# Spreading the S5 parameters over the first feed-forward blocks, and the zeros for the inverses' DRAM blocks over the output stage behind them

## The chip, the cores and the metric

The kernel runs on one core of one Trainium2 chip. The metric is the device time of one execution in microseconds (us). The kernel before was run three times: 1168.38, 1169.02 and 1170.4 us, median 1169.02 us.

## The reference, cut to what matters

One layer of a backbone is computed for 384 tokens of width 1024 (128 context tokens and 256 latent tokens, which share the weights). The order is: norm, SwiGLU feed-forward, norm, a mixer of three branches (S5, SSD, gated DeltaNet), norm, SwiGLU feed-forward, final norm. Each norm's scale and shift and each residual's gate come from an "ada" projection of the condition.

```python
mod = (jax.nn.silu(cond) @ p['ada_w'] + p['ada_b']).reshape(cond.shape[0], 1, N_ADA, D_MODEL)
h = _rmsnorm(x, p['norm_g'][0]) * (1.0 + sc1) + sh1
x = x + 0.5 * g1 * _swiglu(h, p['ffn_wi'][0], p['ffn_wo'][0])
...
# in the S5 branch, from weights alone
dt = jnp.exp(log_dt)[:, None]
mag = jnp.exp(lam_re * dt)
lb_re = mag * jnp.cos(lam_im * dt)
lb_im = mag * jnp.sin(lam_im * dt)
cr = ((lb_re - 1.0) * lam_re + lb_im * lam_im) / den
bb_re = cr[..., None] * b_re - ci[..., None] * b_im
```

The change touches only work that depends on weights and conditions, not on the tokens: these S5 parameters (the powers of the complex decay and the scaled input matrices), the silu of the conditions from which later ada sections are made, and a block of zeros in DRAM which the DeltaNet inverses later fill in part.

## The kernel before, in words

**Matrix products.** Each f32 weight tile of 128 x 1024 is read by DMA into one of three `wraw` buffers and split in two (`split_w`, L279 to L286): ScalarE writes the high part `whi` (L284), VectorE the low part `wlo` (L285). Two buffers each hold `whi` and `wlo`. TensorE makes three products for each 128-row slice (`mm3`, L291 to L293): high by high, high by low, low by high, so 24 matmuls of 384 columns for a weight of 8 slices.

**The first norm** (`modnorm`, L365 to L381) goes through eight slices of the activations in four sections of two. Ahead of a section, `sections` calls `ada_first` (L212 to L233): four DMAs of ada weights (`araw`, L217), matmuls (L221), a copy on ScalarE (L224), transposes (L227), a reduction and an addition on VectorE (L229, L233). Then come `mscale` (L343), the scaled tokens `nt` (L376, VectorE), the high part `hh` (L378, ScalarE) and the low part `hl` (L379, VectorE). The first feed-forward blocks consume slices as they come.

**The first feed-forward** (`ffn`, L389 on) has two parts. In each, 11 blocks m make the two halves of the SwiGLU from two weights (`wi`), multiply (`g`, L409) and split (`gh`, L418; `gl`, L419); m counts from 0 to 21 over both parts. Then an output stage of 8 blocks multiplies with `wo` and adds to x (L431). Behind each block's `gl` stands a call of `fill(m, g)`, behind each output block one of `fill2(part, m)`, both inside `tc.issue_after(last.ins)`: each instruction of VectorE that is traced inside is queued behind that block's last VectorE instruction. Instructions of other engines, and DMA issues on SP's queue, get no such edge.

**Side work in the fills.** `rest` is the generator `ada_rest` (L257 to L274) for three more ada sections. Its first step reads the conditions `cb` (1 MB, broadcast to all partitions, L262), held back by a VectorE copy of one element (L261), and takes their silu on ScalarE (L263). Each of its 24 steps then reads one `araw` (L268) and makes two VectorE products with it (L271). `tables` (`s5_tables`, L549 on) makes eight pairs of S5 tables in two steps each: E (L566 to L572), then B with transposes, matmuls and small copies on top. There are 16 steps.

**Ahead of the fills**, behind the first norm in the program: `zr` is made on GpSimd as zero times the norm's last `hl` (L1337), so that its DMA to `dI` in DRAM (1.5 MB, L1338) can't start earlier; and `s5_params` (L470 to L547) makes the S5 parameters from `smalls` (the second parameter DMA, L1334) by chains of small VectorE instructions on 128 x 32 values, with Exp (L479, L481) and Sin (L494, L497) on ScalarE, reads `braw` and `craw` (L532, L535, each held by a one-element copy of `hl`), and multiplies `bb` (six products of 128 x 512, by `cmul`, L460 to L468).

**Order.** The instructions of each engine stand in an order that is settled when the program is built, by a list scheduler with a model of times: an instruction whose inputs and buffers are there can be placed ahead of others that stand before it in the program. Each engine then works through its order. All DMAs of this stage are issued from SP's one queue.

## Time and profile before

| | |
|---|---|
| median of three runs | 1169.02 us |
| the profiled execution's own time | 1170.72 us |
| its span | 1168.9 us |
| busy: TensorE, VectorE, ScalarE, GpSimd | 1104.1, 807.4, 458.0, 200.3 us |
| mean granted TensorE clock | 0.974 of full speed |
| moved by DMA | 199.21 MB, 170 GB/s over the span |

The span counts from the first to the last instruction of the profiled execution; 1.8 us of its time lie outside. In the rows below PE is TensorE's matmuls and PEld its weight loads, DVE is VectorE, ACT is ScalarE, POOL is GpSimd, SPq is the queue from which SP issues DMAs. A row of the timeline gives the start, the duration, the engine, the line, the operation with output and inputs, the count, and in brackets the idle time of that engine just before, with what ended it. Matmuls are pipelined: each starts before the recorded end of the one before it, so the distance of starts is what one costs.

### The profile page before, as it was taken

What the parts mean: (1) busy time and instruction counts of PE and PEld (TensorE: products, weight loads), DVE (VectorE), ACT (ScalarE), POOL (GpSimd) and SP (SyncE); (2) the same over time, 40 slices, a digit from 0 to 9 for tenths busy, and PEclk for the clock granted to TensorE, in tenths of its full rate; (3) what the DMA queues carried; (4) which work ended last, traced back from release to release, by engine and by line L of the source; (5) the groups of instructions that cost most, each with busy time, mean ns of one, the idle gap of its engine ahead of it and who ended that gap; (6) DMA issues with size and microseconds to landing.
All of it is one profiled execution on the core that took longest, in us unless ns stands there. A gap on an engine that the chain in (4) does not pass through costs nothing.

```text
span 1168.9 us, 19259 instructions
## 1 busy us (share of the span) xinstructions
PE 1104.1 (94%) x7264; PEld 1039.9 (89%) x7264; DVE 807.4 (69%) x1698; ACT 458.0 (39%) x774; POOL 200.3 (17%) x270
## 2 busy tenths in 40 slices
PE   5899999999998999889699999999999999999996
PEld 2689999999998998778588888999899999999996
DVE  4699987997657589954564567775775984455554
ACT  5353333333545573553333222334354433234341
POOL 0000000000000008881372552113500000000000
PEclk9999999999998899989799999999999999999998
DMA  9786767555655353248746444365764644444342
GB/s 355 266 265 213 224 212 234 167 167 161 225 167 145 123 164 112 75 124 245 207 138 216 153 120 125 130 201 163 226 195 145 201 130 122 142 126 127 104 124 80
DMA packets 107342, 199.21 MB, mean 170 GB/s; under 512 B 35056, under 2 KB 61936, under 8 KB 106992
## 3 DMA queue, kind: packets, MB, share of 16 engines
q1 hardware_dynamic: 107248, 197.98, 54.6%
q8 instruction: 57, 0.93, 0.3%
q14 instruction: 37, 0.30, 0.1%
HBM read 175.56 MB, written 22.38 MB: 169 GB/s over the span
## 4 chain that ended last, share of the span: by engine, by line
PE 75%; DVE 12%; DMA 4%; issue 3%; ACT 3%; POOL 2%; SPq 1%; DVEq 0%; ACTq 0%; POOLq 0%
PE ps_d L293 20%; PE ps_d L291 20%; PE ps_d L292 20%; DVE wlo L285 2%; ACT whi L284 1%; DVE sc L818 1%; DMA wraw<-in_win_dram 1%; PE ps_c L1032 1%; PE ps_d L243 1%; PE ps_s L770 1%; PE ps_m L221 1%; PE ps_s L1032 1%; PE ps_m L849 1%; DVE cv L679 1%; DVE Ss L822 1%
## 5 line engine op out<-in xcount | busy, mean ns | idle before, releaser
L284 ACT CAST whi<-wraw 128x1024 fp32r<-128x1024 f32 (+3 forms) x247 | 227.9, 924 | 466.9 <-PE ps_d L292 306.4
L285 DVE TENSOR_TENSOR wlo<-wraw,whi 128x1024 fp32r<-128x1024 f32 (+3 forms) x247 | 276.3, 1119 | 120.8 <-ACT whi L284 119.7
L291 PE MATMUL ps_d<-hh,whi 128*128 128x384 f32 x696 | 243.1, 350 | 16.2 <-ACT whi L284 13.2
L293 PE MATMUL ps_d<-hh,wlo 128*128 128x384 f32 x696 | 243.7, 351 | 5.5 <-DVE wlo L285 5.4
L292 PE MATMUL ps_d<-hl,whi 128*128 128x384 f32 x696 | 242.2, 348 | 0.6 <-DVE hl L379 0.6
L291 PEld LDWEIGHTS ps_d<-hh,whi 128*128 128x128 f32 x696 | 134.4, 193 | 25.9 <-ACT whi L284 16.8
L293 PEld LDWEIGHTS ps_d<-hh,wlo 128*128 128x128 f32 x696 | 135.0, 194 | 12.8 <-DVE wlo L285 9.7
L292 PEld LDWEIGHTS ps_d<-hl,whi 128*128 128x128 f32 x696 | 135.1, 194 | 3.3 <-issue 1.8
L291 PE MATMUL ps_d<-xh,whi 128*128 128x386 f32 x352 | 120.0, 341 | 0.0
L293 PE MATMUL ps_d<-gh,wlo 128*128 128x384 f32 x352 | 119.1, 338 | 1.0 <-DVE wlo L285 1.0
L293 PE MATMUL ps_d<-xh,wlo 128*128 128x386 f32 x352 | 119.9, 341 | 0.0
L291 PE MATMUL ps_d<-gh,whi 128*128 128x384 f32 x352 | 118.8, 337 | 0.4 <-ACT whi L284 0.4
L292 PE MATMUL ps_d<-xl,whi 128*128 128x386 f32 x352 | 118.9, 338 | 0.0
L292 PE MATMUL ps_d<-gl,whi 128*128 128x384 f32 x352 | 118.6, 337 | 0.0
L271 DVE SCALAR_TENSOR_TENSOR ajunk<-araw,cb 128x1024 bf16<-128x1024 f32 x64 | 77.8, 1215 | 1.6 <-ACT cb L263 1.6
L293 PEld LDWEIGHTS ps_d<-gh,wlo 128*128 128x128 f32 x352 | 66.0, 188 | 2.0 <-DVE wlo L285 1.6
L291 PEld LDWEIGHTS ps_d<-gh,whi 128*128 128x128 f32 x352 | 66.1, 188 | 0.9 <-ACT whi L284 0.7
L292 PEld LDWEIGHTS ps_d<-xl,whi 128*128 128x128 f32 x352 | 66.6, 189 | 0.0
L293 PEld LDWEIGHTS ps_d<-xh,wlo 128*128 128x128 f32 x352 | 66.2, 188 | 0.2 <-DVE wlo L285 0.2
L291 PEld LDWEIGHTS ps_d<-xh,whi 128*128 128x128 f32 x352 | 66.3, 188 | 0.0
L292 PEld LDWEIGHTS ps_d<-gl,whi 128*128 128x128 f32 x352 | 66.1, 188 | 0.0
L431 DVE SCALAR_TENSOR_TENSOR x<-ps_d,gate,x 128x128 f32<-128x128 f32 x64 | 23.7, 412 | 29.3 <-PE ps_d L293 29.3
(466 smaller groups left out, 1821.1 us busy)
## 6 DMA issues: line engine op xcount, KB each, us to landing
wraw<-in_wi_dram SPq DMA_DIRECT2D x88, 512.0 KB
wraw<-in_win_dram SPq DMA_DIRECT2D x50, 512.0 KB
araw<-in_ada_dram SPq DMA_DIRECT2D x48, 512.0 KB
wraw<-in_wo_dram SPq DMA_DIRECT2D x32, 384.0 KB
wraw<-in_ada_dram SPq DMA_DIRECT2D x24, 512.0 KB
wraw<-in_wo_dram SPq DMA_DIRECT2D x32, 320.0 KB
wraw<-in_wbr_dram SPq DMA_DIRECT2D x32, 256.0 KB
dM<-sgate SPq DMA_DIRECT2D x24, 192.0 KB
```

Of the source, the lines that this page charges most:

```text
L221: PE.matmul(pt[32 * g:32 * g + 32, :], c32[:, k, :], raw[:, j, :], start=q < 2, stop=q >= 2, tile_position=(0, 32 * g))
L243: PE.matmul(pt[32 * g:32 * g + 32, :], c32[:, 4 * h + g, :], raw[:, g, :], start=h == 0, stop=h == 1, tile_position=(0, 32 * g))
L271: V.scalar_tensor_tensor(junk, raw, 1.0, cb[:, e], op0=ALU.mult, op1=ALU.mult, accum_out=t[:, b, e:e + 1])
L284: S.copy(hi, raw)
L285: V.tensor_tensor(lo, raw, hi.bitcast(F32), op=ALU.subtract)
L291: PE.matmul(pt, hi[:, k, :], xh[k0 + k], start=start and k == 0, stop=False)
L292: PE.matmul(pt, hi[:, k, :], xl[k0 + k], start=False, stop=False)
L293: PE.matmul(pt, lo[:, k, :], xh[k0 + k], start=False, stop=stop and k == nk - 1)
L431: last = V.scalar_tensor_tensor(xv[m][:, s0:s1], py[:, s0:s1], gate[:, m, e:e + 1], xv[m][:, s0:s1], op0=ALU.mult, op1=ALU.add)
L679: V.scalar_tensor_tensor(ol, il, ws, ol, op0=ALU.mult, op1=ALU.add)
L770: PE.matmul(pt[:, ri, g], sw[:, ri, g], UU[:, 4 * b + g], start=True, stop=True)
L1032: PE.matmul(dst[r_, h], lh[r_, h], rh[r_, h] if len(rh.shape) == 3 else rh[r_], start=True, stop=True)
```

## The change

`s5_params` becomes part of the generator `tables`: it is no longer run behind the first norm, but in four steps (three inner `yield`s and one before its return) inside `fill`, ahead of the first table. `tables` now takes a step at every block but m = 11, where it skipped six blocks before. `rest` takes its first eight steps at m = 2 to 9, where they were at m = 0 to 7, and so the conditions' read comes with m = 2. `zr` is set by a plain memset without the norm's `hl` as input. The one DMA of 1.5 MB of zeros becomes four of 384 KB, in `fill2` behind output blocks 0, 2, 4 and 6 of part 0.

```diff
 def s5_params(sp, after):
...
         S.activation(cs, ab, AF.Sin)
+        yield
         pw = sp.tile([P, 2, 10, 32], F32, name="pw")
...
         V.tensor_copy(mu[:, 1, 1], pw[:, 0, 8])
 
+        yield
         den, t1, t2, cr, ci, lm = (t32() for _ in range(6))
...
         cmul(V, bb[:, 0, :, 0:16], bb[:, 1, :, 0:16], braw[:, 0], braw[:, 1], crb, cib, b1, b2)
 
+        yield
         pq = sp.tile([P, 2, 10, 32], F32, name="pq")
...
         V.tensor_copy(pb[64:128], pw[64:128, :, 0:8])
+        yield
         return bb, craw, pq, pb
...
-        zr = s5pool.tile([P, 256], F32, name="zr")
-        G.tensor_scalar(zr, hl[KD - 1][:, 0:256].bitcast(F32), 0.0, None, op0=ALU.mult)
-        nc.sync.dma_start(out=dI.rearrange("t d x h p c -> (t d x h p c)").rearrange("(n p c) -> p n c", p=P, c=256), in_=zr.unsqueeze(1).to_broadcast([P, 12, 256]))
-        tabs = s5_params(s5pool, hl[KD - 1].bitcast(F32))
-
         rest = ada_rest(s5pool, (2, 3, 4), hl[KD - 1].bitcast(F32))
 
         def all_tables():
+            tabs = yield from s5_params(s5pool, hl[KD - 1].bitcast(F32))
             for b in range(8):
                 yield from s5_tables(s5pool, b, *tabs)
 
         tables = all_tables()
+        zr = s5pool.tile([P, 256], F32, name="zr")
+        G.memset(zr, 0.0)
 
         def fill(m, g):
-            if m < 8 or 11 <= m < 19:
+            if 2 <= m < 10 or 11 <= m < 19:
                 next(rest, None)
-            if m not in (0, 5, 9, 11, 16, 20):
+            if m != 11:
                 next(tables, None)
 
         def fill2(part, m):
             if part == 0:
                 next(rest, None)
+                if m % 2 == 0:
+                    m //= 2
+                    nc.sync.dma_start(out=dI.rearrange("t d x h p c -> (t d x h p c)").rearrange("(n p c) -> p n c", p=P, c=256)[:, 3 * m:3 * m + 3],
+                                      in_=zr.unsqueeze(1).to_broadcast([P, 3, 256]))
```

## Rows read from the trace of the kernel before

**Rows 1.** The page, busy time and share of the span of each engine.

```profile
PE 1104.1 (94%) x7264; PEld 1039.9 (89%) x7264; DVE 807.4 (69%) x1698; ACT 458.0 (39%) x774; POOL 200.3 (17%) x270
```

**Rows 2.** Busy time by stretch (length, engines, granted clock, DMA share, GB/s).

```profile
24.00:40.00 16.00, 12.43 (x59) 7.25 (x59) 15.58 (x81) 7.24 (x16) 0.00 (x0) 0.79 0.98 384
...
62.00:141.00 79.00, 75.66 (x492) 74.03 (x493) 77.14 (x121) 32.60 (x50) 0.00 (x0) 1.00 0.75 237
...
190.00:283.00 93.00, 91.11 (x604) 88.78 (x608) 81.18 (x123) 33.46 (x50) 0.00 (x0) 1.00 0.57 177
```

**Rows 3.** Timeline, 20 to 38 us: the first norm's first two sections.

```profile
20.49 0.19 DVE L229 TENSOR_REDUCE at<-ps_m 128x8 f32<-128x32 f32 x1 [5.42 <-PE ps_m L227]
...
21.27 1.40 DVE L376 SCALAR_TENSOR_TENSOR nt<-x,mscale,rb 128x128 f32<-128x128 f32 x4
...
26.18 0.18 DVE L514 TENSOR_TENSOR s5t<-smalls 128x32 f32<-128x32 f32 x1
...
31.22 0.18 DVE L229 TENSOR_REDUCE at<-ps_m 128x8 f32<-128x32 f32 x1
...
32.12 0.23 DVE L233 TENSOR_TENSOR mod<-at,smalls 128x4 f32<-128x4 f32 x2
...
33.14 1.39 DVE L376 SCALAR_TENSOR_TENSOR nt<-x,mscale,rb 128x128 f32<-128x128 f32 x4
...
35.23 0.96 PE L227 MATMUL ps_m<-ident,arows 128*128 128x128 f32 x4
35.73 1.01 DVE L379 SCALAR_TENSOR_TENSOR hl<-nt,mod,hh 128x128 fp32r<-128x128 f32 x3
...
36.53 0.69 PE L292 MATMUL ps_d<-hl,whi 128*128 128x384 f32 x1 [0.34 <-DVE hl L379]
...
37.74 0.49 DVE L544 COPY pq<-pw 64x640 f32<-64x640 f32 x1
```

**Rows 4.** Groups of VectorE by line, 26 to 38.3 us.

```profile
L379 DVE SCALAR_TENSOR_TENSOR hl<-nt,mod,hh 128x256 fp32r<-128x256 f32 (+1 forms) x5 | 2.0, 427 | 0.0
```

**Rows 5.** Timeline, 66 to 78 us: blocks 3 and 4 and the conditions' silu.

```profile
66.34 0.34 PE L291 MATMUL ps_d<-hh,whi 128*128 128x384 f32 x1
...
68.56 0.33 SPq L262 DMA_DIRECT2D cb<-in_condr_dram  x1
...
70.55 0.34 PE L291 MATMUL ps_d<-hh,whi 128*128 128x384 f32 x1
...
74.68 1.91 ACT L263 ACTIVATE cb<-cb 128x2048 f32<-128x2048 f32 x1 [2.62 <-DMA cb<-in_condr_dram]
...
75.13 1.22 DVE L285 TENSOR_TENSOR wlo<-wraw,whi 128x1024 fp32r<-128x1024 f32 x1
...
76.50 1.03 ACT L284 CAST whi<-wraw 128x1024 fp32r<-128x1024 f32 x1
...
77.58 0.44 PE L291 MATMUL ps_d<-hh,whi 128*128 128x384 f32 x1 [2.30 <-ACT whi L284]
```

**Rows 6.** Groups of VectorE by line, 62 to 141 us.

```profile
L285 DVE TENSOR_TENSOR wlo<-wraw,whi 128x1024 fp32r<-128x1024 f32 (+1 forms) x18 | 21.7, 1203 | 4.0 <-ACT whi L284 4.0
...
L566 DVE TENSOR_TENSOR tE<-craw,pq 128x640 f32<-128x640 f32 x6 | 4.7, 818 | 0.0
```

**Rows 7.** Timeline: GpSimd's first memsets, SP's queue to 60 us.

```profile
1.26 1.81 POOL L529 MEMSET bb<- 128x2048 f32 x1
...
12.68 0.33 SPq L1334 DMA_DIRECT2D smalls<-in_small_dram  x1
14.59 7.68 SPq L217 DMA_DIRECT2D araw<-in_ada_dram  x6
...
58.29 0.38 SPq L1338 DMA_DIRECT2D dI<-zr  x1
```

**Rows 8.** Timeline, ScalarE at 24 us: a table load and the Exp behind it.

```profile
24.22 1.28 ACT L479 ACT_TABLE_LOAD   x1
25.51 0.23 ACT L479 ACTIVATE s5t<-smalls 128x32 f32<-128x32 f32 x1
```

## The prediction

> **What bounds the kernel now.** I read the page's busy times first: TensorE is busy 94% of the span [rows 1], so only work that reaches TensorE as idle time counts. Next I read the busy time by stretch. From 62 to 141 us, where blocks m = 3 to 10 run, TensorE is busy 75.66 of 79 us and idle 3.3, and VectorE is busy 77.14: two engines are full there, TensorE only just the fuller one in effect. From 24 to 40 us TensorE is busy 12.43 of 16 us at a granted clock of 0.79, between its two levels of 1.2 and 2.4 GHz, and DMA runs at a 0.98 share [rows 2]. So the start has idle TensorE time to give, and the feed-forward has little VectorE time to take.
>
> The timeline shows what fills VectorE at the start. The S5 chains run from 26.18 to 38.23 us in between the norm's own instructions [rows 3]. Sections 0 and 1 of the norm do the same steps: in section 0 it is 0.78 us from the reduction (20.49) to the first `nt` (21.27); in section 1 it is 1.92 us (31.22 to 33.14), as S5 products stand in between. After `nt` ends at 34.53, `hl` starts only at 35.73, behind S5 copies, and TensorE's product with it waits until 36.53 [rows 3].
>
> **The change, part by part.**
>
> *S5 chains leave the start.* Section 1 gains 1.92 - 0.78 = 1.1 us up to `nt` and 35.73 - 34.53 = 1.2 us behind it: `hl` could be there 2.3 us sooner. TensorE can't follow by all of that: four transposes (35.23, 0.96 us) stand ahead of its product [rows 3] and need the next section's DMA and a ScalarE copy, which moves by 1.1 us with `nt`. I take -1.5 us. The bounds are -2.7 (both VectorE delays and the wait of 0.34 that the row shows) and 0 (the DMA, at a share of 0.98 [rows 2], is late next).
>
> *The same chains enter the feed-forward.* Their stretch of 12.05 us holds 15 instructions of the norm: five `hl` at 2.0 us [rows 4], four `nt` at 1.39 [rows 3], and six small ones at no more than 0.23 each, 0.9 in all. So the S5 part is 12.05 - 4.3 = 7.8 us of VectorE. It now comes behind blocks 0 to 3. Against it, one table step fewer is due by m = 10 (seven steps, was eight). A table step of kind E is six products of 0.82 [rows 6], 4.9 us busy; one of kind B is somewhat less; I take 4. Net +3.8 us, where VectorE has 79 - 77.1 = 1.9 us left [rows 2]: 1.9 us too much. The tables may slip into the output stage, where nobody waits for them; but the order is settled at build time, and a low part that comes late stalls TensorE. I take +1.2, with bounds of 0 (all slips) and +5.9 (all 7.8 less the 1.9).
>
> *The conditions' read moves from block 0 to block 2.* Before, it is issued at 68.56; its silu on ScalarE waits 2.62 us for it and holds the next cast until 76.50; TensorE stands 2.30 us, until 77.58, and VectorE's low part came as late as 75.13 [rows 5]. Moved, the same read and silu hold ScalarE for the same time some blocks later, when a cast has more room: a weight takes TensorE 4.2 us (66.34 to 70.55 [rows 5]), and with two `whi` buffers a cast of 1.03 us may start one weight ahead, so it can be 3.2 us late. I take -1.0, bounds -2.3 and 0. One row of VectorE's queue pays: `braw`, 512 KB, is now asked for right behind the conditions, and the six products wait for it in VectorE's queue, low parts behind them. The read of `cb` took 6.1 us to land (68.56 to 74.68). I take +0.5, bounds 0 and +2.
>
> *Table loads on ScalarE.* Before, one load for Exp, one for Sin, one back to silu. Exp of the step size has no fence and can stay early; then silu, Exp, Sin, silu: two loads more, 2 x 1.28 = 2.6 us [rows 8]. ScalarE is busy 32.6 of 79 us [rows 2], which hides them: 0, bounds 0 and +0.7 (Exp, Sin and silu in a row are 3.85 us, 0.65 over the 3.2 a cast can be late). In the trace a load takes 1.28 us and the Exp starts 0.01 us behind it [rows 8], so the load is the whole price. The Trainium skill (ScalarE: Activation LUTs, "What ACT_TABLE_LOAD costs") puts a switch of sets at about 2.66 us, with a drain beside the load; the trace doesn't show the drain, and by the page the sum would be 3 x 2.66 - 3.2 = 4.8 us longer.
>
> *The zeros.* Before, `zr` waits for the norm and its DMA goes out at 58.29 [rows 7]. Now `zr` needs nothing, and the four DMAs have no other input; the fence of `fill2` binds only VectorE. The program's order lets an instruction without a fence go early: `bb`'s memset, behind the norm in the program, ran at 1.26, and the second parameter read, also behind it, at 12.68, ahead of the next ada reads at 14.59 [rows 7]. So I expect the four DMAs beside that read, not in the output stage. Their 1.57 MB (12 x 128 x 256 values of 4 bytes) at 384 GB/s [rows 2] are 4.1 us of a full DMA stage. What they push back (the ada reads of sections 1 to 3) had some room, since section 1 waited for VectorE. I take +0.6, bounds 0 (room enough, or the DMAs stay in the output stage) and +4.1. Three more issues on SP at 0.38 [rows 7] are 1.1 us beside its waits: 0.
>
> *Part 1* has one table step more, 4 us, where VectorE is busy 81.2 of 93 [rows 2]: 0, bounds 0 and +1.
>
> The sum: -1.5 + 1.2 - 1.0 + 0.5 + 0 + 0.6 + 0 = -0.2 us. The whole order is settled anew, which the trace can't price. Against the profiled execution's 1170.7 us that is 1170.5; it lay 1.7 us over the median of 1169.0, so the forecast is **1168.8 us**.
>
> **The rivals.** A measurement of this kernel tells about 0.2%, 2.3 us, from no change.
>
> *Gain at the start kept, the silu's stall gone, tables slip.* The start gives its -1.5, the stall its -2.3, nothing comes back: 1169.0 - 3.8 = 1165.2 us. For it: VectorE's side work already runs late without TensorE waiting. Against: VectorE is full. Chance 0.36.
>
> *VectorE becomes the bound in blocks 3 to 10.* Place: the low parts of those blocks; price: 7.8 - 1.9 = 5.9 us, less the 1.5 of the start: 1169.0 + 4.4 = 1173.4 us. It decides once a low part ends over 2 us behind its high part's use: 4.2 - 1.03 - 1.2 (a low part [rows 6]). Chance 0.15.
>
> *The zeros don't go where the change puts them, and it costs.* All four reach the queue ahead of the ada reads, and TensorE waits for the full 4.1 us: 1169.0 + 4.1 - 1.5 = 1171.6 us, with more of the start at the low clock. Chance 0.11.
>
> *Drains at table switches*, the page's rule, as a mechanism here: ScalarE held past a cast's room. With a gap like a load's own behind each of three (3 x 2 x 1.28 - 3.2 = 4.5 us): 1168.8 + 4.5 = 1173.3 us. Against it is the 0.01 us gap [rows 8]: chance 0.02. The Trainium skill's figure of the same page would give about the same.
>
> **How the numbers follow.** Forecast 0.36, its own range 1166.7 to 1171.3; the faster rival 0.36; slower ones 0.28 together. So faster 0.36, same 0.36, slower 0.28. The range reaches beyond the faster rival by the other bounds (-2.7 - 2.3 at the start and the silu, 1164.0, and 1 us for the new order) and to the slower ones: 1163 to 1174.5.
>
> **What would show it.** In the changed profile: no S5 rows on VectorE before 60 us, reduction to `nt` near 0.8 us in each section; the product with section 1's `hl` at about 35 us, not 36.53. DMAs of `zr` near 13 us mean the zeros went early; near 141 to 190 us, that I misread the fence. Table loads for Exp and Sin near 66 to 72 us. VectorE idle for TensorE between 62 and 141 would refute the full-VectorE rival; TensorE waiting for `wlo` there would confirm it. The forecast is wrong if the norm's sections wait for DMA, or if TensorE's idle time in blocks 3 to 10 moves from 3.3 us by more than 2.3.

## The result, and the profile after

The changed kernel takes **1178.86 us** (median of 4 runs, 1175.54 to 1181.5) where before takes 1168.92 (4 runs) beside it: a ratio of 1.0079, interval 1.0051 to 1.0106. So it is 9.9 us slower, and the range given (1163 to 1174.5) doesn't hold it. A repeat gave 1.0068, 1.0048 to 1.0087.

The page's busy times of the changed kernel answer to [rows 1]:

```profile
span 1178.1 us, 19258 instructions
...
PE 1113.1 (94%) x7264; PEld 1038.9 (88%) x7264; DVE 800.2 (68%) x1698; ACT 461.1 (39%) x776; POOL 196.3 (17%) x270
```

The shares are those of before, and they tell nothing. By stretch, against [rows 2]:

```profile
24.00:40.00 16.00, 12.56 (x54) 4.85 (x52) 4.25 (x18) 2.77 (x6) 0.00 (x0) 0.98 1.03 414
62.00:141.00 79.00, 75.19 (x478) 71.28 (x477) 76.97 (x165) 36.35 (x53) 0.00 (x0) 1.00 0.65 206
190.00:283.00 93.00, 92.34 (x614) 90.06 (x613) 84.53 (x133) 34.11 (x52) 0.00 (x0) 1.00 0.59 184
```

VectorE has gone from 15.58 to 4.25 us in the start, as the change says, and yet TensorE's weight loads have gone down, from 59 (7.25 us) to 52 (4.85): something else is late there. (Their busy time falls with the granted clock too, which is 0.79 in the first row and 0.98 in the second; their number does not.) From 62 to 141 us PE busy is almost the same (75.66, now 75.19), but weight loads fell from 74.03 to 71.28. A matmul's end is modelled, so a slow stream of matmuls can still look busy; the weight loads, 2.75 us fewer, are the better gauge.

To see where the time went, one landmark per stage is worth more than shares. VectorE writes each output block of the feed-forward into `x` (L431); the first such row ends part 0's blocks, the last ends the feed-forward. First before, then the changed kernel, from VectorE's timeline:

```profile
149.82 0.73 DVE L431 SCALAR_TENSOR_TENSOR x<-ps_d,gate,x 128x128 f32<-128x128 f32 x2
...
340.58 0.74 DVE L431 SCALAR_TENSOR_TENSOR x<-ps_d,gate,x 128x128 f32<-128x128 f32 x2 [0.45 <-PE ps_d L293]
```

```profile
153.04 0.74 DVE L431 SCALAR_TENSOR_TENSOR x<-ps_d,gate,x 128x128 f32<-128x128 f32 x2 [0.17 <-PE ps_d L293]
...
343.93 0.74 DVE L431 SCALAR_TENSOR_TENSOR x<-ps_d,gate,x 128x128 f32<-128x128 f32 x2 [0.45 <-PE ps_d L293]
```

All that the change touches lies ahead of 343.93, and by these rows it costs 3.2 us there up to the first output block and 3.35 us in all. The other 6.6 of the 9.9 us come later, in a stage whose code the change doesn't touch: the mixer. From the feed-forward's end to the mixer's first output row (L1308 in before) it is 506.1 us before, 512.2 and 508.6 in two profiles of the changed kernel, and from there to the end 322.0 to 322.5 in all three.

That split is not quite right, though. The landmarks count from the span's start, and the one profiled execution of before began late. The reduction of the norm's section 0 lies ahead of everything that was edited. It stands at 20.49 in before [rows 3], at 18.06 in the changed kernel, and between 18.33 and 19.67 in the nine kernels of the table whose start is that of before (before_late, before_dummy, before_skip18, before_burst, out_tables0, five_even, five_odd, six_late, before_skip20). The changed kernel, then before_skip18:

```profile
18.06 0.19 DVE L229 TENSOR_REDUCE at<-ps_m 128x8 f32<-128x32 f32 x1 [4.23 <-PE ps_m L227]
```

```profile
18.92 0.19 DVE L229 TENSOR_REDUCE at<-ps_m 128x8 f32<-128x32 f32 x1 [4.91 <-PE ps_m L227]
```

A second landmark, used below, is TensorE's wait for a low part near 62 us, still ahead of the first `fill`. It stands at 62.38 in before and between 59.91 and 61.17 in the nine, 60.7 in the mean. Before, then before_skip18:

```profile
62.38 0.45 PE L293 MATMUL ps_s<-hh,wlo 128*128 128x384 f32 x1 [0.47 <-DVE wlo L285]
```

```profile
60.53 0.44 PE L293 MATMUL ps_s<-hh,wlo 128*128 128x384 f32 x1 [0.46 <-DVE wlo L285]
```

So before's landmarks are some 1.7 us later than its start usually gives, and its own time fits that: the execution took 1170.72 us, 1.7 over the median of the first three runs. By this estimate the loss is nearer to 5 us in the feed-forward and 5 behind it. Both halves had to be explained. In the table the end of the feed-forward is this last L431 row of the one profiled execution, the rest is the median less that, and the class is worked out below. Before's median lay between 1168.92 and 1170.04 in the six comparisons; its row takes 1169.5, and with the execution's own 1170.72 its rest is 830.1. Where an expectation gives the feed-forward's length (FFN, 329.3 us for before), it counts from TensorE's first instruction, at 11.29 us in before and between 9.7 and 10.7 in the other profiles.

| kernel | median us (runs) | ratio to before, 95% | feed-forward ends | rest | order of the mixer |
|---|---|---|---|---|---|
| before | 1169.5 | 1 | 340.58 | 828.9 | A |
| changed | 1178.86 (4) | 1.0051 to 1.0106 | 343.93 | 834.9 | B |
| after_again (the same) | 1177.14 (6) | 1.0048 to 1.0087 | 343.87 | 833.3 | B |
| zeros_only | 1169.56 (12) | 0.9987 to 1.0019 | 339.75 | 829.8 | A |
| params_only | 1173.13 (12) | 1.0014 to 1.005 | 341.60 | 831.5 | B |
| zeros_held | 1174.17 (12) | 1.002 to 1.0051 | 341.47 | 832.7 | B |
| before_late | 1171.0 (12) | 0.9992 to 1.0027 | 336.57 | 834.4 | B |
| before_dummy | 1171.98 (10) | 1.0002 to 1.003 | 338.07 | 833.9 | B |
| before_skip18 | 1168.18 (12) | 0.9966 to 1.0001 | 337.53 | 830.7 | A |
| after_m5 | 1174.87 (9) | 1.0031 to 1.0067 | 344.73 | 830.1 | A |
| before_burst | 1174.04 (12) | 1.0025 to 1.0066 | 345.06 | 829.0 | own |
| out_tables0 | 1175.51 (12) | 1.0021 to 1.0066 | 345.32 | 830.2 | A |
| params_spread | 1171.54 (12) | 0.9995 to 1.0039 | 340.77 | 830.8 | A |
| five_even | 1165.12 (6) | 0.9933 to 0.9968 | 335.01 | 830.1 | A |
| five_odd | 1158.09 (6) | 0.9885 to 0.9938 | 335.10 | 823.0 | C |
| six_late | 1170.13 (12) | 0.9997 to 1.0019 | 342.00 | 828.1 | B |
| after_m9 | 1171.64 (12) | 0.9995 to 1.0036 | 344.43 | 827.2 | C |
| before_skip20 | 1169.8 (12) | 0.9976 to 1.0017 | 336.18 | 833.6 | B |
| params_third | 1163.87 (12) | 0.9935 to 0.9965 | 337.31 | 826.6 | C |

### The profile page after: what moved, and what is told of

It reads as the page before. It is cut to its first block, busy times and chain, and to the rows that moved or that the text cites. A ratio compares the mean times of both kernels' runs of the same rounds, so it can differ in the third digit from the quotient of the medians.

```text
span 1178.1 us, 19258 instructions
## 1 busy us (share of the span) xinstructions
PE 1113.1 (94%) x7264; PEld 1038.9 (88%) x7264; DVE 800.2 (68%) x1698; ACT 461.1 (39%) x776; POOL 196.3 (17%) x270
## 4 chain that ended last, share of the span: by engine, by line
PE 76%; DVE 10%; DMA 4%; ACT 3%; issue 3%; POOL 2%; SPq 2%; DVEq 0%; ACTq 0%; POOLq 0%
PE ps_d L293 20%; PE ps_d L291 20%; PE ps_d L292 20%; DVE wlo L285 2%; ACT whi L284 1%; PE ps_d L243 1%; PE ps_c L1036 1%; DMA wraw<-in_win_dram 1%; PE ps_m L221 1%; DVE sc L822 1%; PE ps_m L853 1%; PE ps_s L774 1%; DVE ajunk L271 1%; DMA araw<-in_ada_dram 1%; PE ps_s L1036 1%
## 5 line engine op out<-in xcount | busy, mean ns | idle before, releaser
L285 DVE TENSOR_TENSOR wlo<-wraw,whi 128x1024 fp32r<-128x1024 f32 (+3 forms) x247 | 273.0, 1106 | 127.3 <-ACT whi L284 123.9
L291 PE MATMUL ps_d<-hh,whi 128*128 128x384 f32 x696 | 241.7, 348 | 11.5 <-ACT whi L284 9.3
L293 PE MATMUL ps_d<-hh,wlo 128*128 128x384 f32 x696 | 242.3, 349 | 5.8 <-DVE wlo L285 5.6
L291 PEld LDWEIGHTS ps_d<-hh,whi 128*128 128x128 f32 x696 | 133.4, 192 | 22.9 <-ACT whi L284 13.0
L293 PEld LDWEIGHTS ps_d<-hh,wlo 128*128 128x128 f32 x696 | 133.5, 192 | 12.1 <-DVE wlo L285 9.8
L291 PE MATMUL ps_d<-gh,whi 128*128 128x384 f32 x352 | 119.0, 339 | 1.2 <-ACT whi L284 1.2
L291 PE MATMUL ps_d<-xh,whi 128*128 128x386 f32 x352 | 119.9, 341 | 0.0
L293 PE MATMUL ps_d<-xh,wlo 128*128 128x386 f32 x352 | 119.8, 340 | 0.0
L293 PE MATMUL ps_d<-gh,wlo 128*128 128x384 f32 x352 | 118.7, 338 | 0.7 <-DVE wlo L285 0.7
L291 PEld LDWEIGHTS ps_d<-gh,whi 128*128 128x128 f32 x352 | 66.1, 188 | 2.6 <-ACT whi L284 2.5
L293 PEld LDWEIGHTS ps_d<-gh,wlo 128*128 128x128 f32 x352 | 66.0, 188 | 2.0 <-DVE wlo L285 1.6
L293 PEld LDWEIGHTS ps_d<-xh,wlo 128*128 128x128 f32 x352 | 66.2, 188 | 0.1
L291 PEld LDWEIGHTS ps_d<-xh,whi 128*128 128x128 f32 x352 | 66.3, 188 | 0.0
```

The source lines that it names most:

```text
L285: V.tensor_tensor(lo, raw, hi.bitcast(F32), op=ALU.subtract)
L291: PE.matmul(pt, hi[:, k, :], xh[k0 + k], start=start and k == 0, stop=False)
L293: PE.matmul(pt, lo[:, k, :], xh[k0 + k], start=False, stop=stop and k == nk - 1)
```

## The experiments: the change taken apart

**The zeros alone.** The kernel before, with nothing but the zeros changed as in the diff.

```diff
-        zr = s5pool.tile([P, 256], F32, name="zr")
-        G.tensor_scalar(zr, hl[KD - 1][:, 0:256].bitcast(F32), 0.0, None, op0=ALU.mult)
-        nc.sync.dma_start(out=..., in_=zr.unsqueeze(1).to_broadcast([P, 12, 256]))
...
+        G.memset(zr, 0.0)
...
             if part == 0:
                 next(rest, None)
+                if m % 2 == 0:
+                    m //= 2
+                    nc.sync.dma_start(out=...[:, 3 * m:3 * m + 3], in_=zr...)
```

> The kernel before with the zeros alone as in the changed kernel (memset without input, four DMAs behind output blocks 0, 2, 4 and 6); the S5 parameters stay behind the first norm. The order of the mixer's instructions is the same as before on every engine. If the zeros' early DMAs are what the feed-forward loses (3.3 us of the changed kernel's loss lie before the mixer), this kernel is 2 to 4 us slower than before. If the S5 chains on VectorE are, it is within 1 us of before, as the ada reads have room.

**The rest alone.** The changed kernel, with the zeros as before.

```diff
+        G.tensor_scalar(zr, hl[KD - 1][:, 0:256].bitcast(F32), 0.0, None, op0=ALU.mult)
+        nc.sync.dma_start(out=..., in_=zr.unsqueeze(1).to_broadcast([P, 12, 256]))
...
-        G.memset(zr, 0.0)
...
-                if m % 2 == 0:
-                    m //= 2
-                    nc.sync.dma_start(out=...[:, 3 * m:3 * m + 3], in_=zr...)
```

> The S5 parameters and the conditions' read as in the changed kernel; the zeros as before (one DMA, held by the norm's last slice). The order of the mixer is that of the changed kernel on every engine. If the zeros cost nothing, it is as slow as the changed kernel, some 1178 us; if the zeros' early DMAs cost 2 to 4 us, some 1175 us.

**The zeros really held** until part 0's output stage: VectorE's memset of `zr` put under the fence of `fill2`.

```diff
-        G.memset(zr, 0.0)
...
+                if m == 0:
+                    V.memset(zr, 0.0)
                 if m % 2 == 0:
```

> The changed kernel with the zeros truly held: the memset is made by VectorE inside the block behind output block 0, so all four DMAs wait for it and go out from about 150 us. If the early DMAs cost 2 to 4 us, 1174 to 1176 us; if they cost nothing, as slow as the changed kernel.

**The changed kernel once more**, in the same batch as zeros_held, with no edit:

> The changed kernel again, unaltered, so that it stands beside the kernel before in the same rounds as the next three. If the three parts found so far add up (zeros early 2.5 us, S5 chains in the blocks 2 us, the mixer's order 4 us): 8 to 9 us over before, 1177 to 1179 us.

Measured: zeros_only 1169.56, no different from before; params_only 1173.13; zeros_held 1174.17; the changed kernel again 1177.14. The zeros cost nothing that can be told alone and 4 to 5 us on top of the rest (ratios of 1.0068 and 1.0079 with them, of 1.0032 and 1.0035 without or held back; intervals in the table). The traces say why. The changed kernel's SP queue:

```profile
11.40 0.33 SPq L1338 DMA_DIRECT2D smalls<-in_small_dram  x1
12.78 2.87 SPq L1362 DMA_DIRECT2D dI<-zr  x3
16.61 2.98 SPq L217 DMA_DIRECT2D araw<-in_ada_dram  x2
19.64 0.63 SPq L1362 DMA_DIRECT2D dI<-zr  x1
20.42 4.48 SPq L217 DMA_DIRECT2D araw<-in_ada_dram  x4
```

The four writes don't go out in the output stage, some 140 us later, where their line stands: three are issued at 12.78, ahead of the reads for the next sections of the norm (16.61; 14.59 in [rows 7]). What that does is on TensorE's and VectorE's timeline of the changed kernel, against [rows 3]; first the norm's steps, then TensorE's waits:

```profile
30.52 0.19 DVE L229 TENSOR_REDUCE at<-ps_m 128x8 f32<-128x32 f32 x1 [6.69 <-PE ps_m L227]
...
31.22 1.41 DVE L376 SCALAR_TENSOR_TENSOR nt<-x,mscale,rb 128x128 f32<-128x128 f32 x4
...
32.54 1.40 DVE L379 SCALAR_TENSOR_TENSOR hl<-nt,mod,hh 128x128 fp32r<-128x128 f32 x4
```

```profile
26.73 1.05 PE L221 MATMUL ps_m<-araw,c 128*32 128x512 f32 x4 [1.34 <-DMA araw<-in_ada_dram]
28.03 1.05 PE L221 MATMUL ps_m<-araw,c 128*32 128x512 f32 x4 [0.26 <-DMA araw<-in_ada_dram]
...
33.34 0.45 PE L292 MATMUL ps_d<-hl,whi 128*128 128x384 f32 x1 [0.16 <-DVE hl L379]
...
62.84 0.44 PE L293 MATMUL ps_s<-hh,wlo 128*128 128x384 f32 x1 [0.47 <-DVE wlo L285]
```

Section 1's way from the reduction to `nt` is now 0.70 us where it was 1.92 [rows 3]; VectorE stands idle for 6.69 us before it, so the norm has a new limit: the read of `araw`, which TensorE awaits for 1.34 and 0.26 us. Without the zeros that wait isn't there; params_only:

```profile
32.11 0.44 PE L292 MATMUL ps_d<-hl,whi 128*128 128x384 f32 x1 [0.17 <-DVE hl L379]
...
60.20 0.44 PE L293 MATMUL ps_s<-hh,wlo 128*128 128x384 f32 x1 [0.46 <-DVE wlo L285]
```

The product with section 1's `hl` comes at 36.53 before [rows 3] (34.40 to 35.71 in the nine kernels with its start), at 33.34 with the change and at 32.11 without its zeros. The last row of either fence is the landmark near 62 us: 62.38 before, 60.20 in params_only, 62.84 with the change. In zeros_held, where the writes do wait for the output stage (152.2 us), it is 59.71.

Read from before's own profile, the S5 chains' leaving gives 2.2 us. That is too much, as that profile is late: four kernels without the S5 chains in the start and without early zeros (params_only, zeros_held, params_spread, params_third) have the landmark at 59.9 in the mean, the nine with the chains at 60.7 (the ranges, 59.34 to 60.41 and 59.91 to 61.17, overlap). So some 0.8 us are left at the landmark of the 3.2 by which section 1's product comes earlier (31.85 and 35.05 in the mean); where the rest goes stays open. The zeros, ahead of the reads, take 2.6 us: 60.20 to 62.84. The three kernels of the change with early zeros have the landmark at 62.84 (after_again 62.85), 63.15 (after_m9) and 65.06 (after_m5), the four without between 59.34 and 60.41.

In zeros_only TensorE awaited `araw` as well, and section 1's product came later than in before and in any of the nine:

```profile
27.14 3.17 PE L221 MATMUL ps_m<-araw,c 128*32 128x512 f32 x8 [1.05 <-DMA araw<-in_ada_dram]
...
37.91 0.69 PE L292 MATMUL ps_d<-hl,whi 128*128 128x384 f32 x1
```

Most of that was made good later: the stall of 2.30 us for the conditions' silu [rows 5] is gone, and from 62 to 100 us TensorE waits for one low part alone:

```profile
PE ps_d L293 <- DVE wlo L285: 0.4, 1, 0.4
```

The two edits interact: the wait in which the zeros alone were hidden is the one for the silu, and the rest of the change removes it, as it moves the conditions' read.

## The experiments: VectorE in blocks 3 to 10

From that landmark to the first output block it is 87.4 us before (149.82 - 62.38) and 90.2 in the changed kernel (153.04 - 62.84), in params_only (150.40 - 60.20) and in zeros_held. Both ends are taken from one profile, so a late start doesn't matter here. 2.8 us are lost, although the stall for the conditions' silu (2.30 us at 77.58 [rows 5]) is gone. VectorE's timeline of the changed kernel shows the place where the S5 chains bunch, and TensorE's row behind it:

```profile
77.09 1.22 DVE L285 TENSOR_TENSOR wlo<-wraw,whi 128x1024 fp32r<-128x1024 f32 x1
...
79.51 0.68 DVE L461 TENSOR_TENSOR tt<-braw,s5t 128x512 f32<-128x512 f32 x1
80.11 0.69 DVE L463 TENSOR_TENSOR bb<-braw,s5t 128x512 f32<-128x512 f32 x1
80.72 0.68 DVE L464 TENSOR_TENSOR tt<-braw,s5t 128x512 f32<-128x512 f32 x1
81.32 1.22 DVE L271 SCALAR_TENSOR_TENSOR ajunk<-araw,cb 128x1024 bf16<-128x1024 f32 x1
...
84.63 1.22 DVE L285 TENSOR_TENSOR wlo<-wraw,whi 128x1024 fp32r<-128x1024 f32 x1
```

```profile
85.90 0.44 PE L293 MATMUL ps_d<-hh,wlo 128*128 128x384 f32 x1 [0.51 <-DVE wlo L285]
```

A weight needs a low part every 4.2 us [rows 5]; here one ends at 78.31 and the next starts at 84.63, behind more than 6 us of S5 copies, `bb` products and one ada product.

What that place costs can be read by counting TensorE's matmuls of L291 to L293 in either timeline from the landmark on. The 103rd behind it starts 18.19 us later in the changed kernel and 20.74 before: 2.5 us gained, what the silu's stall was worth, and up to there, past the added table loads, the changed kernel's TensorE shows no wait. The 128th starts at 24.22 and 25.12: of the gain 0.9 is left, so the bunch cost some 1.7 us. The 428th starts at 84.86 and 83.64: another 2.1 us went in small pieces in the blocks behind, where the changed kernel takes seven table steps (blocks 4 to 10) and before takes five. That these steps are what costs it there is argued and not shown: the profile's waits for low parts and high parts between 62 and 141 us add up to 3.8 us where before has 3.5.

Two experiments ask whether it is the amount of VectorE work or its place that costs. The first adds ten dependent products of 128x32, results unused, behind each of blocks 0 to 3, 40 in all.

```diff
...
         def fill(m, g):
+            if m < 4:
+                for _ in range(10):
+                    V.tensor_tensor(dum[:, 1], dum[:, 0], dum[:, 1], op=ALU.mult)
```

> The kernel before with 40 useless VectorE products of 128 x 32, ten behind each of blocks 0 to 3, each waiting for the last (8 us of VectorE, about what the S5 chains take), and nothing moved. It leaves no part of the computation out. If the changed kernel's loss in the blocks is VectorE's time, the first output stage begins 2 to 4 us later than in the kernel before; if it is the table loads or the late reads, it begins as before, within 1 us. The mixer's order is that of the changed kernel here, so its time as a whole is judged up to the feed-forward's end alone.

It did not do what it was meant to. The products take 0.18 us each, and the built order strewed them singly from 66.7 to 167.8 us, some 4 us apart at first: 20 of them, 3.6 us, lie between 62 and 141 us, not 8. The stage got no longer by them: from the landmark (60.70) to the first output block (146.46) it is 85.8 us, 1.7 less than before, which neither theory expected. The time rose by 2.5 us (1171.98; 1.0002 to 1.003), and that lies behind the feed-forward (the table: 833.9), of which more below. The second experiment puts one burst in one place:

```diff
...
         def fill(m, g):
+            if m == 2:
+                for i in range(4):
+                    V.tensor_reduce(dum[:, i], g.unsqueeze(1).to_broadcast([P, 4, T]), axis=AX.X, op=ALU.add)
```

> The kernel before, with four extra reductions of 128x4x384 on VectorE behind block 2, results unused, which stand in one piece ahead of a low part. At the 1.2 us that VectorE needs for 1024 elements in the profile of before they are some 1.8 us each, 7 us in all, about the 7.8 us of the S5 chains. Theory (a burst of VectorE work ahead of a low part, in the stretch where VectorE is full, comes back as TensorE idle time, less the slack): first output-block update 2.5 to 5 us later than in before, from the end of section m2b's low-part wait, and the time 2 to 5 us up. Rival (VectorE work in the blocks costs nothing here, as the 40 small products behind blocks 0 to 3 suggested): stretch unchanged within 1 us, time within 1 us of before.

VectorE's timeline of before_burst, and the one row on TensorE that answers:

```profile
72.39 6.72 DVE L1353 TENSOR_REDUCE dum<-g 128x4 f32<-128x1536 f32 x4
79.03 1.28 DVE L566 TENSOR_TENSOR tB<-bb,pb 128x512 f32<-128x512 f32 x2
80.23 1.22 DVE L285 TENSOR_TENSOR wlo<-wraw,whi 128x1024 fp32r<-128x1024 f32 x1
```

```profile
81.50 0.69 PE L293 MATMUL ps_d<-hh,wlo 128*128 128x384 f32 x1 [4.67 <-DVE wlo L285]
```

6.72 us in front of a low part come back as one stall of 4.67. The first output block is 4.5 us later than before (154.36), 6.1 counted from the landmark (60.84), more than expected; the time is 4.0 us over the 1170.04 of before beside it. So a burst ahead of a low part is paid for the most part. As the burst is also more work than the 3.6 us of the first experiment, the two don't part place from amount.

**Table steps.** The other load in these blocks are the table steps. Four kernels vary only the blocks at which a step is drawn:

```diff
 before_late
-            if m not in (0, 5, 9, 11, 16, 20):
+            if m in (1, 2, 3, 4, 6, 7, 8) or 12 <= m <= 20:
 before_skip18
-            if m not in (0, 5, 9, 11, 16, 20):
+            if m not in (0, 5, 9, 10, 11, 18):
 after_m5
-            if m != 11:
+            if m not in (5, 11):
 out_tables0
-            if m not in (0, 5, 9, 11, 16, 20):
+            if m in (1, 3, 6, 8, 12, 13, 14, 15, 16, 17, 18, 19):
...
                 next(rest, None)
+                if m in (1, 3, 5, 7):
+                    next(tables, None)
```

> The kernel before, with nothing moved but the table steps of the later blocks: nine steps at m = 12 to 20, as in the changed kernel, instead of one at m = 10 and eight at 12 to 21. S5 parameters and zeros stay where they were. The mixer's order comes out as that of the changed kernel. Theory A, that the changed kernel's loss in the mixer (5.7 us between 474 and 800 us) comes from the mixer's order and not from anything that was moved: 1173 to 1176 us, with the loss behind 470 us. Theory B, that the moved work itself costs it (tables later, another state of the queues): 1168 to 1170 us.

> The kernel before with table steps skipped at m = 10 and 18 in place of 16 and 20. The mixer's order is almost that of before; the table steps between blocks 10 and 21 come as late as in the earlier run that skipped 10 and 21 and whose feed-forward ended 4 us sooner. Theory A: the feed-forward's 3 to 4 us are kept, with nothing lost in the mixer: 1165 to 1166.5 us. Theory B: no gain, 1169 us.

> The changed kernel with one table step skipped, at m = 5; all later steps come one block later. The mixer's order comes out almost as that of the kernel before (0.99 of it alike), while zeros and S5 parameters are where the change puts them. Theory A (the order of the mixer costs 4 to 5 us by itself): 4 to 5 us faster than the changed kernel, with the gain between the feed-forward's end and the reload of the gates. Theory B (the order is as good, the moved work costs it): as slow as the changed kernel.

> The kernel before, with table steps in blocks 1, 3, 6 and 8 alone, four more in part 0's output stage and the other eight in blocks 12 to 19; the later stage keeps nearly the order of before. Theory (each table step taken out of the full stretch gives some 1 to 3 us of the first eight blocks, the output stage has VectorE time to take it, and the mixer keeps its time): FFN 326 to 328 us where before has 329.3, time 1166 to 1168.5. Rival (all gains of this kind are below what can be told): 1168.5 to 1170.

With one step less in the eleven blocks it is 85.2 us (before_late) and 85.4 (before_skip18) from the landmark to the first output block, 2.0 to 2.2 less than before; on the changed kernel 85.7 (after_m5, from 65.06 to 150.73), 4.5 less, of which part 1 took most back (279.7 to the feed-forward's end, 281.1 unedited). In before_skip18 the time did not follow: 1168.18, no different from before, where 1165 to 1166.5 was expected. And before_dummy gained nearly as much (85.8) with no step less, so it isn't the number of steps as such; which placements are good was not worked out. out_tables0 missed: the first output block came 6.5 us earlier (143.28), but the output stage, from the first block to the eighth, took 50.9 us, where before takes 41.6 (149.82 to 191.43). Its timeline of TensorE shows low parts late there too:

```profile
154.65 0.44 PE L293 MATMUL ps_d<-gh,wlo 128*128 128x384 f32 x1 [1.16 <-DVE wlo L285]
```

The same is true of params_spread, which takes the change without its zeros, gives each step a block of its own and puts six steps into the output stage:

```diff
-            if m != 11:
+            if m in (0, 2, 4, 5, 7, 9, 12, 13, 14, 15, 16, 17, 18, 19):
...
                 next(rest, None)
+                if m in (0, 2, 3, 5, 6, 7):
+                    next(tables, None)
```

> The changed kernel with the zeros as in the kernel before, table and S5 steps taken singly at blocks 0, 2, 4, 5, 7, 9, six in part 0's output stage and eight in blocks 12 to 19, and the later stage in nearly the order of before. Theory (the change loses by bunched VectorE work in the blocks, by the zeros ahead of the sections' reads, and by the mixer's new order; with all three taken away the gain at the start of some 2 us is left): from m2b's low-part wait to the first output-block update 86 to 88 us (params_only 90.2), time 1165.5 to 1168.5, under before. Rival (the S5 chains cost their full VectorE time wherever they stand in the feed-forward): 1169.5 to 1172.

It has the earliest first output block of all (139.98), an output stage of 50.9 us, and 1171.54 in the end, where 1165.5 to 1168.5 was expected: a miss as well. The output stage has no room for such steps. Part 1 has some: in five_even, below, its blocks take 109.0 us with eleven steps (183.26 to 292.22) where before takes 106.7 with eight (191.43 to 298.17).

## The experiments: the mixer, which nobody touched

The order in which each engine takes its instructions is settled when the program is built, and a step moved in the feed-forward settles the mixer's anew. Compared as sequences, from 335 to 800 us, VectorE's instructions in the traces fall into classes: within one they agree to 0.97 or more (1 is the same sequence), between two to 0.87 at most. The kernel before and the changed one are in two of them, A and B, and agree to 0.85. A third, C, agrees to about 0.64 with A. Does the rest behind the feed-forward go with the class? Two of the kernels above were meant to tell, and both fell between their theories: before_late at 1171.0 (1173 to 1176 if the order costs, 1168 to 1170 if not), and after_m5 2.3 us under the changed kernel beside it (4 to 5, or nothing). Three more tests were made: five_even against five_odd, which draw five steps in part 0 and eleven in part 1; six_late and before_skip20, kernels without the change in the changed kernel's order; and after_m9, the changed kernel in the third order.

```diff
 five_even
-            if m not in (0, 5, 9, 11, 16, 20):
+            if m in (2, 4, 6, 8, 10, 11, 12, 13, 14, 15, 16, 17, 18, 19, 20, 21):
 five_odd
-            if m not in (0, 5, 9, 11, 16, 20):
+            if m in (1, 3, 5, 7, 9, 11, 12, 13, 14, 15, 16, 17, 18, 19, 20, 21):
 six_late
-            if m not in (0, 5, 9, 11, 16, 20):
+            if m in (1, 2, 4, 6, 8, 9, 11, 12, 13, 14, 15, 16, 17, 18, 19, 20):
 before_skip20
-            if m not in (0, 5, 9, 11, 16, 20):
+            if m not in (0, 5, 9, 10, 11, 20):
 after_m9
-            if m != 11:
+            if m not in (9, 11):
```

> The kernel before with table steps in blocks 2, 4, 6, 8, 10 and 11 to 21 (five in the eleven blocks of part 0 where before has eight, eleven in part 1 where before has eight). Its mixer has nearly the order of before. Theory (a step out of the full blocks gives 1 to 2.8 us, a step into part 1's blocks costs about 0.7, the mixer stays): first output-block update near 143, FFN 323 to 327 us (before 329.3), time 1164 to 1168. Rival (part 1 has no VectorE time left for three more steps, and gives it all back): FFN 328 to 331, time 1168.5 to 1171.

> As five_even, with the steps of part 0 in blocks 1, 3, 5, 7, 9. The feed-forward should be within 2 us of five_even's; the mixer stands in a third order. Theory (the order of the mixer has a price of its own, of some 3 us): the time differs from five_even's by 2 us or more beyond the feed-forward's difference. Rival (the mixer's length varies by chance, not by order): the difference of the times is that of the feed-forwards within 1.5 us.

> The kernel before with table steps in blocks 1, 2, 4, 6, 8, 9 and 11 to 20; the mixer stands in the order of the changed kernel, while nothing of the change itself is in it. Theory (that order costs some 3 us in the mixer): FFN 324 to 328 us and time 1167.5 to 1171.5, that is 2 to 4 us over what its feed-forward gives against before's 1169.5. Rival (order without price): time 1169.5 less the feed-forward's gain, within 1.5 us.

> The kernel before with the table step of block 10 moved to block 16, as before_skip18, but with part 1's pause at block 20 instead of 18. The mixer stands in the changed kernel's order instead of that of before. Theory (that order costs 2 to 4 us): feed-forward within 1 us of before_skip18's 327.3, time 1170 to 1172.5. Rival (those two orders cost the same): 1167 to 1169.5.

> The changed kernel with one table step less by block 10 (none behind block 9), which puts the mixer into the third order, that of five_odd. Theory (the order has a price of its own): the feed-forward ends near 342 to 345 us as in the changed kernel (343.9), and from there it takes 823 us as in five_odd, so 1165 to 1168, under before, with every part of the change in it. Rival (what five_odd gained came from something else): 1173 to 1178, as after_m5, which has one step less as well.

**five_even and five_odd** end the feed-forward within 0.1 us of each other (335.01, 335.10), 5.5 us earlier than before, and finish 7.0 us apart, at 1165.12 and 1158.09. In the program nothing differs behind it but the order. It is six runs each, and the intervals just touch (0.9933 to 0.9968, 0.9885 to 0.9938).

**The changed kernel in three orders**: unedited (B), without the step behind block 5 (A), without the one behind block 9 (C). The feed-forward ends at 343.9, 344.7 and 344.4; the times are 1178.86 and 1177.14, 1174.87, and 1171.64. In the third order the whole change stands at 1.0016 (0.9995 to 1.0036) of before, an interval below the unedited kernel's, though not as low as expected (1165 to 1168).

**before_skip18 and before_skip20** differ in one step of part 1: the second ends its feed-forward 1.35 us earlier and the run 1.6 us later, as expected in sign, but their intervals overlap (0.9966 to 1.0001, 0.9976 to 1.0017), so the pair alone shows nothing. **six_late** is the miss: it is in order B, and its rest is the shortest of that class, 828.1; its feed-forward, expected at 324 to 328 us long, took 331.9 (to 342.00), so the number of steps in the blocks isn't the whole of that either.

Over the classes the rest is 830.1 us in A (seven kernels, 828.9 to 830.8), 832.8 in B (eight medians, the changed kernel's two among them, 828.1 to 834.9, all but six_late over 831) and 825.6 in C (three, 823.0 to 827.2). Of the 5 us behind the feed-forward the order explains some 3 by the means; the changed kernel's own medians lie higher in their class (834.1 in the mean), and how much of that is more than scatter stays open.

One rival is left for order C: the granted clock. Over whole runs its median is 0.980 to 0.981 in C's three kernels, 0.974 to 0.977 in A and 0.976 to 0.977 in B, and the time goes with it, loosely: over the 29 runs of before 0.01 more clock goes with about 6 us less (correlation -0.59). By that slope, an estimate, the clock would make some 3 of the 4.5 us between A and C. Whether C's order brings the higher clock or only happened to meet it, no run tells. Between A and B the clock is the same.

Where in the mixer? The busy times from 450 to 600 us, in the order before, changed, after_m9, five_odd:

```profile
450.00:600.00 150.00, 128.08 (x984) 114.61 (x983) 99.98 (x277) 60.49 (x102) 92.85 (x159) 0.91 0.54 159
```

```profile
450.00:600.00 150.00, 125.05 (x920) 110.49 (x920) 94.33 (x276) 58.43 (x100) 80.50 (x155) 0.94 0.55 156
```

```profile
450.00:600.00 150.00, 130.21 (x975) 113.69 (x973) 96.22 (x276) 61.55 (x105) 86.30 (x156) 0.94 0.57 166
```

```profile
450.00:600.00 150.00, 134.05 (x1077) 115.89 (x1075) 95.40 (x258) 60.95 (x102) 89.27 (x144) 0.95 0.58 174
```

TensorE is idle for 21.9, 25.0, 19.8 and 16.0 us there. These four alone would make B the worst and C the best, but over all profiles the stretch sorts only C from A: A has 21.9 to 27.1 us, B 18.6 to 25.0 (22.2 in the changed kernel's second profile), C 16.0 to 20.8. TensorE's waits in the same stretch (total, times, longest), for before, the changed kernel and after_m9:

```profile
PE ps_s L967 <- POOL Hc L947: 5.4, 1, 5.4
...
PE ps_s L1032 <- POOL Lm L1040: 1.0, 1, 1.0
```

```profile
PE ps_s L971 <- POOL Hc L951: 4.9, 1, 4.9
...
PE ps_s L1036 <- POOL Lm L1044: 3.3, 1, 3.3
```

```profile
PE ps_s L1036 <- DMA X<-dI: 3.0, 1, 3.0
...
PE ps_s L971 <- ACT th L862: 2.4, 1, 2.4
```

In every profile of A and B TensorE waits for one GpSimd result, `Hc`, for 3.4 to 6.1 us; in C it is 2.0 in five_odd and not in the list of the other two, and what after_m9 waits for in its place is shorter. That may be what C gains; it isn't shown. The wait for `Lm` doesn't go with the order: 3.3 us in the changed kernel, none in its second profile, 2.4 in out_tables0 (A) and 3.0 in params_third (C). Where B loses against A stays open.

**The best of both.** The S5 chains out of the start, the zeros as before, two steps less in part 0, one more in part 1, and the third order:

```diff
 params_only
-            if m != 11:
+            if m not in (3, 4):
```

> The changed kernel with the zeros as in the kernel before, no step behind blocks 3 and 4 and one behind each of the others; the mixer stands in the third order. Theory: S5 chains out of the start give their 2 us, two steps less in part 0 some 2 to 5, so the feed-forward ends at 335 to 339, and 823 us more give 1158 to 1162. Rival: with the S5 chains in part 0 the feed-forward ends at 341 as in params_only, and the time is 1164 or more.

It takes 1163.87 us, a ratio of 0.995 (0.9935 to 0.9965), a little over its range, and beats before and the changed kernel. five_odd, with the S5 chains left in the start, is the fastest run here: 1158.09, ratio 0.9911 (0.9885 to 0.9938). The page of five_odd:

```profile
span 1152.6 us, 19258 instructions
...
PE 1099.4 (95%) x7264; PEld 1030.9 (89%) x7264; DVE 803.2 (70%) x1698; ACT 458.9 (40%) x774; POOL 199.4 (17%) x270
```

## Why the prediction was wrong

It gave 1168.8, and 1178.86 came: 9.9 us over before, where the sum was -0.2. By its steps:

| step | forecast, us | measured, us | from |
|---|---|---|---|
| S5 chains leave the start | -1.5 (-2.7 to 0) | -0.8 | means of the landmark, 60.7 to 59.9 |
| zeros | +0.6 (0 to +4.1) | +2.6 | params_only to the changed kernel, 60.20 to 62.84 |
| S5 chains, `braw`, conditions' read in blocks 3 to 10 | +1.2 + 0.5 - 1.0 = +0.7 | +2.8 | 87.4 to 90.2 |
| output stages and part 1 | 0 | +0.1 | 190.8 (340.58 - 149.82) to 190.9 |
| the order settled anew | 0 | +5.2 | what the four rows leave of 9.9 |

*The start* was right in its mechanism: the section's steps fell from 1.92 to 0.70 us, and the product came even earlier than the 35 us forecast. Of that 0.8 us was left at the landmark, half of the term. The prediction's own sign of being wrong came true there: with the zeros in front, the sections of the norm wait for DMA.

*The zeros* went where the prediction said they would, near 13 us and not in the output stage. The term was mis-sized, within its bounds: "what they push back had some room, since section 1 waited for VectorE" is the step that failed. In zeros_only, with VectorE's chains in place, section 1 had no such room, as its product came at 37.91; what hid the zeros there was the later stall for the silu, which the prediction itself took away under another term. With that stall gone they cost 2.6 us.

*The blocks.* That VectorE is full and that a late low part stalls TensorE was right, and the rival built on it came true in part. The size failed: +2.8 us where +0.7 was taken. Net VectorE time less spare VectorE time over a stretch of 79 us took no account of where the work lands: more than 6 us of it came between two low parts and cost some 1.7 there. As the stall of 2.30 us for the silu did go, all that came in took some 5 us gross (2.8 + 2.3) where 1.7 (1.2 + 0.5) was taken; the greater part went in the blocks behind the bunch, and its cause stays open. The prediction's other sign, TensorE's idle time in these blocks moving by more than 2.3 us, did not show it: that went from 3.3 to 3.8.

*Table loads* were right: the loads for Exp, Sin and back to silu stand at 66.55, 69.45 and 72.84. ScalarE's timeline of the changed kernel:

```profile
69.45 1.28 ACT L494 ACT_TABLE_LOAD   x1
70.74 0.23 ACT L494 ACTIVATE s5t<-s5t 128x32 f32<-128x32 f32 x1
...
72.84 1.28 ACT L408 ACT_TABLE_LOAD   x1
74.13 0.50 ACT L408 ACTIVATE sa<-ps_d 128x384 f32<-128x384 f32 x1
```

1.28 us, and the next activation 0.01 us behind, as in [rows 8]. The figure of the Trainium skill (ScalarE: Activation LUTs, "What ACT_TABLE_LOAD costs"), about 2.66 us with its drain, shows at neither load.

*The order* is the step that failed most, a term put at nothing. "The whole order is settled anew, which the trace can't price" was followed by 0 in the sum and 1 us in the range. The experiments give a size: between the means of the classes seen here lie 7 us, of which the clock may have a share in C's. The change happened to leave A for B, 2.7 us slower by the means, and stood high within B; 5.2 of the 9.9 us lie behind the feed-forward. What makes B slow in the mixer stays open. With five us or so on each side, the range would have held the result.

## What to carry to other kernels

When a move changes an order that a builder settles anew, give the order a term and a range of its own, and try a neighbouring placement before the change is judged: here the change with one table step less (after_m9) took 5.5 to 7 us less than without that edit. Before a wait is called room for something else, ask whether the same change removes it. On a full engine look at what would stand between two pieces of work that another engine awaits, and not only at the engine's spare time over the stage. And before two profiles are compared by the clock of the span, compare a row that lies ahead of every edit.

## What the runs showed that was not expected

Two profiles of the changed kernel end the feed-forward at 343.93 and 343.87 us, with their first output blocks both at 153.04. Their totals, 1179.90 and 1176.68, differ by 3.2 us, all of it behind that point. That looks as if a landmark told part of a microsecond, but ten profiles with one and the same start (before and the nine kernels named above) have section 0's reduction anywhere from 18.33 to 20.49 us. Counted from the span's start, a landmark of one profile tells about 2 us, no more than the median of a dozen runs does.

Behind the feed-forward the scatter goes in part with TensorE's granted clock. zeros_only and before stand in the same order; from 345 to 847 us their profiles have a mean clock of 0.97 and 0.96, and it is 500.5 and 506.1 us from the feed-forward's end to the mixer's first output row. Of the 29 runs of before the fastest, 1161.65, had a mean clock of 0.979, the slowest, 1174.99, one of 0.972.

In the start, from 24 to 40 us, the granted clock is a mean between the levels of 1.2 and 2.4 GHz in before (0.79) and near the higher one in the changed kernel (0.98). The change doesn't show as the cause: the nine kernels with before's start have 0.76 to 0.95 there, and after_m5, with every part of the change, 0.63. Nor did the higher clock bring more matmuls into the stretch, 54 and not 59; TensorE's waits for `araw` stand there instead.
